# A hybrid encoder block on one core: first token tile ahead at the step into the MLP, a shared start of four up-projection blocks, and a last sum partly on TensorE

## The chip, the cores and the metric

The kernel runs as one program on one core of a Trainium2 chip. The metric is the device time of one execution in microseconds (us). TensorE is called PE in the rows below (PEld is its weight load), VectorE DVE, ScalarE ACT, GpSimd POOL, SyncE SP.

## The reference

One residual block is computed for 256 tokens of 2048 channels. It has three sub-layers, each with a norm before it (scale each token by the inverse root mean square) and a norm of its result before the residual sum: token mixers (gated DeltaNet and pooling), cross-attention into 256 memory tokens, and a gated MLP. The change touches the end of the second and the third:

```python
y = memory_cross_attention(h, m, w_xq, w_xkv, w_xo)     # last step: o @ w_xo
x = x + rms_norm(y, xa_post_norm)
h = rms_norm(x, ffn_pre_norm)
u = causal_dwconv(h @ w_up, ffn_conv_w) + ffn_conv_b    # w_up: 2048 x 11008
a, b = jnp.split(u, 2, axis=-1)
y = (jax.nn.silu(a) * b) @ w_down                       # w_down: 5504 x 2048
x = x + rms_norm(y, ffn_post_norm)
```

## The kernel before

All products take float32 data that is split into two parts of fewer bits (a high and a low one); a product is then two or three matmuls. Weights are loaded by SP in chunks of 128 x 2048 (`raw`, three buffers). ACT copies the high part of 1024 columns (`whi`, L154) and DVE subtracts it (`wlo`, L155); of each part there are three buffers, so that this runs ahead of TensorE by at most three pieces of 1024 columns. Each engine takes its instructions in one order that was fixed when the program was built. A scheduler chose that order, except for instructions that are given to `pin`, which stay in the order in which the code writes them.

`proj_tm` makes a block of 512 output channels for both tiles of 128 tokens, three matmuls of 512 columns for each 128 input channels (L195 to L197). The four output blocks of cross-attention are made by it (`xo0` to `xo3`), and after each `PostNorm.block` squares the product on ACT with a sum for each token (L276) and multiplies it by the gain on DVE (L381). After the fourth, `scales` takes the sum to the power -0.5 on POOL (L393, L395), and `piece` adds the residual in quarters of 512 channels on DVE (L400), into `py_xa`. `transpose_in` turns each quarter into channel-major form by 8 transposes on TensorE (L246, two PSUM tiles `tp_h`), and ACT and DVE read these tiles, ACT for the high and DVE for the low part (L253, L255), into `h3T`. That gives the input of the MLP's up-projection in four quarters.

`proj_cm` makes a block of 128 channels of the up-projection for all 256 tokens: 16 pairs of matmuls of 512 and 256 columns (L171, L174). `up` takes blocks in the order 0, 43, 1, 44 and so on (`ua` and `ub`), and adds, scales by the token factors `R3`, convolves, and multiplies. The token factors come from eight squares of `py_xa` (`j_h`), one power for each token tile and a matmul that spreads them over the partitions (`Rp`, then `R`). PSUM has four tiles for the products of `proj_tm` and `proj_cm` (pool `acc`) and four for all else.

The last block of the down-projection, `dn3`, has `tail=3`: over its last six rows of 128 channels the first token tile goes first, and `ff_end` for it runs under the second one's matmuls. `ff_end` for the second tile ends the program with four pieces on DVE and their stores.

Of the kernel before, what the change touches and what calls it, by code (L numbers as in the profile page):

```python
# [25 lines left out]
def kernel(  # L26
    ctx: ExitStack,
    tc: tile.TileContext,
    x: bass.AP,          # [256, 2048]
    x_cm: bass.AP,       # [2, 128, 8, 256]  x, channel-major  # L30
    mem_cm: bass.AP,     # [2, 128, 8, 256]
    w_cm: bass.AP,       # [57, 128, 2048]   (q,k,v per head; b/a; p), channel-major blocks
    w_z: bass.AP,        # [4, 128, 16, 512]
    w_ga: bass.AP,       # [4, 128, 16, 512]
    w_gb: bass.AP,       # [4, 128, 16, 512]
    w_ya: bass.AP,       # [4, 128, 16, 512]
    w_yb: bass.AP,       # [4, 128, 8, 512]
    w_mo: bass.AP,       # [4, 128, 16, 512]
    w_pool: bass.AP,     # [128, 2048]       (c | group, out block, in block, d)
    w_xq: bass.AP,       # [16, 128, 2048]  # L40
    w_xk: bass.AP,       # [16, 128, 2048]
    w_xv: bass.AP,       # [4, 128, 16, 512]
    w_xo: bass.AP,       # [4, 128, 16, 512]
    w_up: bass.AP,       # [86, 128, 2048]
    w_dn: bass.AP,       # [4, 128, 43, 512]
    conv_w: bass.AP,     # [128, 48, 4]
    ffn_w: bass.AP,      # [128, 86, 3]
    ffn_b: bass.AP,      # [128, 86]
    pregain: bass.AP,    # [128, 4, 16]      (mix, xa, mem, ffn)
    postgain: bass.AP,   # [3, 128, 2048]  # L50
    gdn_gain: bass.AP,   # [128, 1]
    pool_sc: bass.AP,    # [128, 8]
    ab: bass.AP,         # [16, 2]           (a_log, dt_bias)
    c_ident: bass.AP,    # [128, 128]
    c_le: bass.AP,       # [128, 128]        1 where partition <= column
    c_gt: bass.AP,       # [128, 128]        1 where partition > column
    c_tinit: bass.AP,    # [128, 256]
    c_invc: bass.AP,     # [128, 64]
    out: bass.AP,        # [256, 2048]
# [126 lines left out]
    def proj_tm(wsrc, X, KT, name, tail=0, mid=None):  # L186
        """out [128 tokens, 512] for both token tiles; over the last 2 * tail rows of
        128 the first token tile goes first, and mid(its product) follows it."""
        ps = [ps_acc(f"tm{t}_{name}") for t in range(NT)]

        def mm(t, k, wh, wl):
# [1007 lines left out]
```

## Time and profile before

| what | value |
|---|---|
| time, median of 3 runs | 2026.81 us (2026.27 to 2026.9) |
| span of the profiled execution, first to last instruction | 2026.0 us |
| PE busy | 2001.8 us, 99% of the span |
| DVE, ACT busy | 1386.6 us (68%), 1099.6 us (54%) |
| mean granted TensorE clock | 0.997 of full speed |
| chain that ended last, by engine | PE 95%, DVE 1% |

The span is that of the one profiled execution; what lies around it is 0.3 to 0.9 us by the three timed runs. Granted clock 1.00 is 2.4 GHz and 0.50 is 1.2 GHz. Busy times overlap, so that shares do not add up to one. A matmul's duration in a row reaches beyond the start of the next one, since matmuls are pipelined.

### The profile page before, as it was taken

What the parts mean: (1) busy time and instruction counts of PE and PEld (TensorE: products, weight loads), DVE (VectorE), ACT (ScalarE), POOL (GpSimd) and SP (SyncE); (2) the same over time, 40 slices, a digit from 0 to 9 for tenths busy, and PEclk for the clock granted to TensorE, in tenths of its full rate; (3) what the DMA queues carried; (4) which work ended last, traced back from release to release, by engine and by line L of the source; (5) the groups of instructions that cost most, each with busy time, mean ns of one, the idle gap of its engine ahead of it and who ended that gap; (6) DMA issues with size and microseconds to landing.
All of it is one profiled execution on the core that took longest, in us unless ns stands there. A gap on an engine that the chain in (4) does not pass through costs nothing.

```text
span 2026.0 us, 27927 instructions
## 1 busy us (share of the span) xinstructions
PE 2001.8 (99%) x10842; PEld 1703.1 (84%) x10842; DVE 1386.6 (68%) x2171; ACT 1099.6 (54%) x1826; POOL 108.5 (5%) x154
## 2 busy tenths in 40 slices
PE   8999999999999999999999999999999999999998
PEld 6888888888878888888888888788888888888886
DVE  7869687697756855678555554688888887854444
ACT  7657666566654544456444444565555555544443
POOL 1510200201100000001000000100000000000000
PEclk9999999999999999999999999999999999999999
DMA  6445354444444656456555455555555555565553
GB/s 242 166 167 183 132 184 147 160 173 146 166 170 153 236 193 249 173 199 228 185 190 175 159 207 190 204 209 187 190 189 192 193 193 187 187 231 200 188 196 141
DMA packets 55029, 377.87 MB, mean 187 GB/s; under 512 B 6768, under 2 KB 7536, under 8 KB 10224
## 3 DMA queue, kind: packets, MB, share of 16 engines
q1 hardware_dynamic: 52128, 359.73, 51.0%
q0 software_dynamic: 2192, 15.73, 2.0%
q8 instruction: 85, 1.39, 0.3%
q10 hardware_dynamic: 576, 0.62, 0.1%
q14 instruction: 48, 0.39, 0.1%
HBM read 369.77 MB, written 6.29 MB: 186 GB/s over the span
## 4 chain that ended last, share of the span: by engine, by line
PE 95%; DVE 1%; POOL 0%; ACT 0%; issue 0%; DVEq 0%; POOLq 0%; ACTq 0%
PE cm_ub L171 8%; PE cm_ua L171 8%; PE cm_ub L174 4%; PE cm_ua L174 4%; PE tm_dn L197 4%; PE tm_dn L196 4%; PE tm_dn L195 4%; PE cm_xk L171 3%; PE cm_xq L171 3%; PE cm_vg L171 3%; PE cm_kg L171 2%; PE cm_qg L171 2%; PE tm_gb L195 2%; PE cm_xk L174 1%; PE cm_xq L174 1%; PE tm_gb L196 1%
## 5 line engine op out<-in xcount | busy, mean ns | idle before, releaser
L171 PE MATMUL cm_ua<-h3T,whi_ua 128*128 128x512 f32 x688 | 242.0, 395 | 0.0
L171 PE MATMUL cm_ub<-h3T,whi_ub 128*128 128x512 f32 x688 | 241.0, 394 | 0.0
L174 PE MATMUL cm_ua<-h3T,wlo_ua 128*128 128x256 f32 x688 | 191.0, 278 | 0.0
L174 PE MATMUL cm_ub<-h3T,wlo_ub 128*128 128x256 f32 x688 | 190.7, 277 | 0.1
L155 DVE TENSOR_TENSOR wlo_dn<-raw_dn,whi_dn 128x1024 fp32r<-128x1024 f32 (+1 forms) x88 | 105.6, 1200 | 119.0 <-ACT whi_dn L154 118.8
L154 ACT CAST whi_dn<-raw_dn 128x1024 fp32r<-128x1024 f32 (+1 forms) x88 | 91.1, 1035 | 136.9 <-PE tm_dn L197 132.2
L171 PEld LDWEIGHTS cm_ua<-h3T,whi_ua 128*128 128x128 f32 x688 | 129.3, 188 | 29.8 <-ACT h3T L253 0.2
L171 PEld LDWEIGHTS cm_ub<-h3T,whi_ub 128*128 128x128 f32 x688 | 129.1, 188 | 29.9
L155 DVE TENSOR_TENSOR wlo_ub<-raw_ub,whi_ub 128x1024 fp32r<-128x1024 f32 x86 | 105.3, 1225 | 58.1 <-ACT whi_ub L154 58.0
L154 ACT CAST whi_ub<-raw_ub 128x1024 fp32r<-128x1024 f32 x86 | 90.4, 1051 | 100.3 <-issue 51.5
L154 ACT CAST whi_ua<-raw_ua 128x1024 fp32r<-128x1024 f32 x86 | 90.6, 1053 | 99.2 <-PE cm_ub L171 47.5
L195 PE MATMUL tm_dn<-whi_dn,gT 128*128 128x512 f32 x344 | 133.8, 389 | 0.0
L196 PE MATMUL tm_dn<-wlo_dn,gT 128*128 128x512 f32 x344 | 133.8, 389 | 0.0
L197 PE MATMUL tm_dn<-whi_dn,gT 128*128 128x512 f32 x344 | 133.8, 389 | 0.0
L174 PEld LDWEIGHTS cm_ub<-h3T,wlo_ub 128*128 128x128 f32 x688 | 129.2, 188 | 0.4 <-DVE wlo_ub L155 0.4
L174 PEld LDWEIGHTS cm_ua<-h3T,wlo_ua 128*128 128x128 f32 x688 | 129.5, 188 | 0.0
L155 DVE TENSOR_TENSOR wlo_ua<-raw_ua,whi_ua 128x1024 fp32r<-128x1024 f32 x86 | 105.3, 1225 | 26.6 <-ACT whi_ua L154 26.5
L171 PE MATMUL cm_vg<-uT,whi_vg 128*128 128x512 f32 x256 | 95.1, 409 | 0.0
L171 PE MATMUL cm_kg<-uT,whi_kg 128*128 128x512 f32 x256 | 93.7, 406 | 0.0
L171 PE MATMUL cm_xk<-meT,whi_xk 128*128 128x512 f32 x256 | 89.7, 396 | 0.0
L171 PE MATMUL cm_xq<-h2T,whi_xq 128*128 128x512 f32 x256 | 88.8, 394 | 0.0
L171 PE MATMUL cm_qg<-uT,whi_qg 128*128 128x512 f32 x240 | 86.4, 401 | 0.0
(412 smaller groups left out, 5350.2 us busy)
## 6 DMA issues: line engine op xcount, KB each, us to landing
raw_ua<-in_w_up_dram SPq DMA_DIRECT2D x43, 1024.0 KB, 4.8
raw_ub<-in_w_up_dram SPq DMA_DIRECT2D x43, 1024.0 KB, 4.8
raw_dn<-in_w_dn_dram SPq DMA_DIRECT2D x40, 1024.0 KB, 4.7
raw_zg<-in_w_z_dram SPq DMA_DIRECT2D x16, 1024.0 KB, 4.8
raw_ga<-in_w_ga_dram SPq DMA_DIRECT2D x16, 1024.0 KB, 4.8
raw_gb<-in_w_gb_dram SPq DMA_DIRECT2D x16, 1024.0 KB, 4.7
raw_ya<-in_w_ya_dram SPq DMA_DIRECT2D x16, 1024.0 KB, 4.8
raw_mo<-in_w_mo_dram SPq DMA_DIRECT2D x16, 1024.0 KB, 4.7
```

Source lines behind the costliest of these rows:

```text
L154: pin(nc.scalar.copy(hi[:, :m], raw[:, s:s + m]), keep)
L155: pin(nc.vector.tensor_tensor(out=lo[:, :m], in0=raw[:, s:s + m], in1=hi[:, :m].bitcast(F32), op=ALU.subtract), keep)
L171: nc.tensor.matmul(ps, lhsT=hi[:, j * P:(j + 1) * P], rhs=xk.rearrange("p a s -> p (a s)"), start=(kt == 0), stop=False)
L174: nc.tensor.matmul(ps[:, 0:S], lhsT=lo[:, j * P:(j + 1) * P], rhs=xk[:, 0, :], start=False, stop=(kt == 15))
L195: nc.tensor.matmul(ps[t], lhsT=xh, rhs=wh, start=(k == 0), stop=False)
L196: nc.tensor.matmul(ps[t], lhsT=xh, rhs=wl, start=False, stop=False)
L197: nc.tensor.matmul(ps[t], lhsT=xl, rhs=wh, start=False, stop=(k == KT - 1))
```

## The change

The loop over the output blocks of cross-attention ends after three. The weights of the first three shared pieces of the up-projection (`up_split`, each 512 columns of two blocks) are then loaded and split, and the fourth block `xo3` is made with `tail=3`. `first_token_tile` normalises the first token tile after its last matmul, and `late` puts its transposes ahead of the last six matmuls of the second. The up-projection's blocks 0, 43, 1 and 44 (`FIRST_UP`) are then made together, quarter by quarter of `h3T`, in four PSUM tiles `cm_up_st0` to `cm_up_st3`; in the first quarter each token tile has its own split and its own matmuls. The squares for the token factors stand after all four quarters. Nearly all of it is pinned. In `ff_end` of the second token tile, the first 512 channels are summed by two matmuls and copied by ACT; DVE keeps three pieces. `square_sum`, `block` and `piece` get an argument `keep` that pins them. Comments and docstrings are removed.

```diff
+    def proj_tm(wsrc, X, KT, name, tail=0, mid=None, late=None):
...
-        def mm(t, k, wh, wl):
+        def mm(t, k, wh, wl, keep=False):
...
-            nc.tensor.matmul(ps[t], lhsT=xh, rhs=wh, start=(k == 0), stop=False)
+            pin(nc.tensor.matmul(ps[t], lhsT=xh, rhs=wh, start=(k == 0), stop=False), keep)
...
         if tail:
             parts = list(chunks(K0, KT))
             for t in range(NT):
-                for part in parts:
-                    for args in part:
-                        mm(t, *args)
+                for i, p in enumerate(parts):
+                    for args in p:
+                        mm(t, *args, keep=True)
                     tick()
+                    if t and late and i == tail - 2:
+                        late()
                 if t == 0:
                     mid(ps[0])
         return ps
...
     pn = PostNorm(1, lambda t: x1[t * P:(t + 1) * P, :], "xa")
-    for nb in range(4):
+    for nb in range(3):
         pn.block(proj_tm(w_xo[nb], A, 16, f"xo{nb}"), nb)
...
     x2 = dram.tile([S, D], F32, name="x2")
-    pn.scales()
     ss = new_ss("h3")
-    h3T = []
-    for q in range(4):
-        ys = [pn.piece(t, q) for t in range(NT)]
-        d = xtile(f"h3T{q}")
-        transpose_in(d, lambda t: ys[t], pre_sb[:, 3, 4 * q:4 * q + 4], f"h3{q}")
-        h3T.append(d)
+    h3T = [xtile(f"h3T{q}") for q in range(4)]
+    H3 = getX(h3T)
+
...
+    FIRST_UP = (0, KFF, 1, KFF + 1)
+    up_parts = []
+
+    def up_split(half):
+        raw = wp.tile([P, 2048], F32, tag="raw", name=f"raw_up_st{half}")
+        c = half // 2
+        for b in range(2):
+            nc.sync.dma_start(raw[:, b * 512:(b + 1) * 512],
+                              w_up[FIRST_UP[2 * (half % 2) + b]][:, c * 512:(c + 1) * 512])
+        hl = b8(f"wup_st{half}", F32R)
+        hi, lo = hl[:, 0:1024], hl[:, 1024:2048]
+        pin(nc.scalar.copy(hi, raw[:, 0:1024]))
+        pin(nc.vector.tensor_tensor(out=lo, in0=raw[:, 0:1024], in1=hi.bitcast(F32),
+                                    op=ALU.subtract))
+        up_parts.append((hi, lo))
+
+    h3tp = {}
...
+    def h3_transpose(q, t):
+        for pr in range(2):
+            if (q, pr) not in h3tp:
+                h3tp[q, pr] = ps_g(f"tp_h3{q}_{pr}")
+            for kk in range(2):
+                o = kk * S + t * P
+                c = q * 512 + (2 * pr + kk) * P
+                pin(nc.tensor.transpose(h3tp[q, pr][:, o:o + P], pn.y[t][:, c:c + P], ident))
+
...
+    def h3_split(q, lo, hi):
+        for k in range(4):
+            gk = pre_sb[:, 3, 4 * q + k:4 * q + k + 1]
+            src = h3tp[q, k // 2][:, k % 2 * S + lo:k % 2 * S + hi]
+            d = h3T[q][:, k]
+            pin(nc.scalar.activation(d[:, 0, lo:hi], src, AF.Identity, scale=gk))
+            pin(nc.vector.scalar_tensor_tensor(out=d[:, 1, lo:hi], in0=src, scalar=gk,
+                                               in1=d[:, 0, lo:hi].bitcast(F32),
+                                               op0=ALU.mult, op1=ALU.subtract))
+
+    def first_token_tile(ps):
+        pn.block([ps] * 2, 3, [0], True)
+        pn.scales([0])
+        pn.piece(0, 0, True)
...
+    ps_up = []
+    def up_mm(half, toks):
+        c = half // 2
+        hi, lo = up_parts[half]
+        for b in range(2):
+            p2 = ps_up[2 * (half % 2) + b].rearrange("p (a s) -> p a s", a=2)
+            for k in range(4):
+                kt = 4 * c + k
+                xk = H3(kt)
+                w = slice(b * 512 + k * P, b * 512 + (k + 1) * P)
+                pin(nc.tensor.matmul(p2[:, :, toks], lhsT=hi[:, w], rhs=xk[:, :, toks],
+                                     start=(kt == 0 and toks.start == 0), stop=False))
+                pin(nc.tensor.matmul(p2[:, 0, toks], lhsT=lo[:, w], rhs=xk[:, 0, toks],
+                                     start=False, stop=(kt == 15)))
+            tick()
+
+    for half in range(3):
+        up_split(half)
+    ps = proj_tm(w_xo[3], A, 16, "xo3", 3, first_token_tile, lambda: h3_transpose(0, 0))
+    ps_up.extend(ps_acc(f"cm_up_st{i}") for i in range(4))
+    h3_split(0, 0, P)
+    pn.piece(0, 1, True)
+    for half in range(2):
+        up_mm(half, slice(0, P))
+    pn.block(ps, 3, [1], True)
+    pn.scales([1])
+    pn.piece(1, 0, True)
+    h3_transpose(0, 1)
+    h3_split(0, P, S)
+    for half in range(2):
+        up_mm(half, slice(P, S))
+    for q in range(1, 4):
         for t in range(NT):
-            square_sum(ys[t], ss[t][:, q:q + 1], f"h3{t}{q}")
+            if t or q > 1:
+                pn.piece(t, q, True)
+            h3_transpose(q, t)
+        h3_split(q, 0, S)
+        for half in (2 * q, 2 * q + 1):
+            if half + 1 < 8:
+                up_split(half + 1)
+            up_mm(half, slice(0, S))
     for t in range(NT):
         nc.gpsimd.dma_start(x2[t * P:(t + 1) * P, :], pn.y[t])
-    H3 = getX(h3T)
+        for q in range(4):
+            square_sum(pn.y[t][:, q * 512:(q + 1) * 512], ss[t][:, q:q + 1], f"h3{t}{q}",
+                       True)
...
     R3, _ = row_factors(ss, "h3")
...
     def up(blk, name):
-        ps = proj_cm(w_up[blk], H3, name)
+        if blk in FIRST_UP:
+            ps = ps_up[FIRST_UP.index(blk)]
+        else:
+            ps = proj_cm(w_up[blk], H3, name)
         xp = next_xp()
...
     def ff_end(t, ps):
         pn.block([ps] * 2, 3, [t])
         pn.scales([t])
+        if t:
+            po = ps_g("last")
+            nc.tensor.matmul(po, lhsT=ident, rhs=pn.x[1][:, 0:512], start=True, stop=False)
+            dr = tmp.tile([P, P], F32, tag="t", bufs=3, name="dr")
+            nc.scalar.activation(dr, ident, AF.Identity, scale=pn.r[1][:, 0:1])
+            nc.tensor.matmul(po, lhsT=dr, rhs=pn.y[1][:, 0:512], start=False, stop=True)
         for q in range(4):
-            y = pn.piece(t, q)
+            if t and q == 0:
+                y = tmp.tile([P, 512], F32, tag="j512", name="y_last")
+                nc.scalar.copy(y, po)
+            else:
+                y = pn.piece(t, q)
             eng = nc.sync if q % 2 == 0 or t == 0 else nc.scalar
             eng.dma_start(out[t * P:(t + 1) * P, q * 512:(q + 1) * 512], y)
```

The order of the built programs shows what moved. On ACT, at the step from `xo2` to `xo3`, there stood before (`whi_xo3_0_0` is the high part of the first 1024 weight columns of `xo3`, `j_xa20` and `j_xa21` are the squares of the products of `xo2` for the two token tiles):

```order
L154 CAST whi_xo2_12_1024_11343<-raw_xo2_12_11337 128x1024
L154 CAST whi_xo3_0_0_11385<-raw_xo3_0_11383 128x1024
L154 CAST whi_xo3_0_1024_11389<-raw_xo3_0_11383 128x1024
L276 ACTIVATE j_xa20_11371,pss_xa0_10926<-tm0_xo2_11233 128x512
L276 ACTIVATE j_xa21_11374,pss_xa1_10927<-tm1_xo2_11234 128x512
L154 CAST whi_xo3_4_0_11419<-raw_xo3_4_11417 128x1024
```

and now:

```order
L154 CAST whi_xo2_12_1024_11343<-raw_xo2_12_11337 128x1024
L278 ACTIVATE j_xa20_11371,pss_xa0_10926<-tm0_xo2_11233 128x512
L278 ACTIVATE j_xa21_11374,pss_xa1_10927<-tm1_xo2_11234 128x512
L1082 CAST wup_st0_11391<-raw_up_st0_11388 128x1024
L1082 CAST wup_st1_11397<-raw_up_st1_11394 128x1024
L1082 CAST wup_st2_11403<-raw_up_st2_11400 128x1024
L154 CAST whi_xo3_0_0_11410<-raw_xo3_0_11408 128x1024
L154 CAST whi_xo3_0_1024_11414<-raw_xo3_0_11408 128x1024
```

The three shared pieces stand ahead of the first piece of `xo3`, and the two squares, which need the last matmuls of `xo2`, stand ahead of these; DVE has the same order for the low parts.

On PE, in the step into the MLP, before (`tp_h31_0` is the first PSUM tile of quarter 1, `py_xa0` the first token tile, `cm_ua0` the product of block 0):

```order
L246 MATMUL tp_h31_1_11571<-ident_82,py_xa0_10922 128x128
L246 MATMUL tp_h31_1_11571<-ident_82,py_xa1_10923 128x128
L171 MATMUL cm_ua0_11666<-h3T0_11536,whi_ua0_0_11669 128x512
L174 MATMUL cm_ua0_11666<-h3T0_11536,wlo_ua0_0_11670 128x256
L171 MATMUL cm_ub0_11718<-h3T0_11536,whi_ub0_0_11721 128x512
L246 MATMUL tp_h32_0_11587<-ident_82,py_xa0_10922 128x128
L171 MATMUL cm_ua0_11666<-h3T0_11536,whi_ua0_0_11669 128x512
L174 MATMUL cm_ua0_11666<-h3T0_11536,wlo_ua0_0_11670 128x256
L246 MATMUL tp_h32_1_11596<-ident_82,py_xa0_10922 128x128
```

and now, at the step from quarter 0 to quarter 1:

```order
L1127 MATMUL cm_up_st3_11562<-h3T0_11384,wup_st1_11397 128x128
L1096 MATMUL tp_h31_0_11655<-ident_82,py_xa0_10922 128x128 x2
L1096 MATMUL tp_h31_1_11658<-ident_82,py_xa0_10922 128x128 x2
L1096 MATMUL tp_h31_0_11655<-ident_82,py_xa1_10923 128x128 x2
L1096 MATMUL tp_h31_1_11658<-ident_82,py_xa1_10923 128x128 x2
L1125 MATMUL cm_up_st0_11559<-h3T1_11385,wup_st2_11403 128x512
L1127 MATMUL cm_up_st0_11559<-h3T1_11385,wup_st2_11403 128x256
```

Before, matmuls of one quarter stood between the transposes of the next ones; now all products of a quarter stand ahead of the next quarter's transposes, and the products of that quarter directly behind them.

On DVE, at the last quarter, before (`s1_h30` sums the squares of a token tile, `dg_h30` puts its factor on a diagonal, `ua_ua0` adds up the product of block 0):

```order
L266 TENSOR_REDUCE s1_h31_11647<-nss_h31_11533 128x1
L155 TENSOR_TENSOR wlo_ub0_1024_11726<-raw_ub0_11719,whi_ub0_1024_11725 128x1024
L255 SCALAR_TENSOR_TENSOR h3T3_11611<-tp_h33_0_11612,pre_sb_80,h3T3_11611 128x256
L255 SCALAR_TENSOR_TENSOR h3T3_11611<-tp_h33_1_11621,pre_sb_80,h3T3_11611 128x256
L302 TENSOR_SCALAR dg_h30_11643<-ident_82,rstd_h30_11638 128x128
L302 TENSOR_SCALAR dg_h31_11651<-ident_82,rstd_h31_11646 128x128
L307 COPY R_h3_11636<-Rp_h3_11637 128x256
L155 TENSOR_TENSOR wlo_ua1_0_11776<-raw_ua1_11773,whi_ua1_0_11775 128x1024
L155 TENSOR_TENSOR wlo_ua1_1024_11780<-raw_ua1_11773,whi_ua1_1024_11779 128x1024
L184 TENSOR_TENSOR ua_ua0_11709<-cm_ua0_11666,t_ua0_11710 128x256
```

and now:

```order
L1105 SCALAR_TENSOR_TENSOR h3T3_11387<-tp_h33_0_11783,pre_sb_80,h3T3_11387 128x256 x2
L1105 SCALAR_TENSOR_TENSOR h3T3_11387<-tp_h33_1_11786,pre_sb_80,h3T3_11387 128x256
L155 TENSOR_TENSOR wlo_ua2_0_11932<-raw_ua2_11929,whi_ua2_0_11931 128x1024
L1105 SCALAR_TENSOR_TENSOR h3T3_11387<-tp_h33_1_11786,pre_sb_80,h3T3_11387 128x256
L1083 TENSOR_TENSOR wup_st7_11805<-raw_up_st7_11802,wup_st7_11805 128x1024
L268 TENSOR_REDUCE s1_h30_11861<-nss_h30_11382 128x1
L304 TENSOR_SCALAR dg_h30_11865<-ident_82,rstd_h30_11860 128x128
L268 TENSOR_REDUCE s1_h31_11869<-nss_h31_11383 128x1
L304 TENSOR_SCALAR dg_h31_11873<-ident_82,rstd_h31_11868 128x128
L155 TENSOR_TENSOR wlo_ua2_1024_11936<-raw_ua2_11929,whi_ua2_1024_11935 128x1024
L309 COPY R_h3_11858<-Rp_h3_11859 128x256
L184 TENSOR_TENSOR ua_ua0_11888<-cm_up_st0_11559,t_ua0_11889 128x256
```

The first weight piece of the fifth block, `wlo_ua2_0`, stands inside the last quarter's split, and its second piece ahead of `R_h3` and of the sum that frees the first of the four PSUM tiles.

## Rows read from the trace of the kernel before

**Rows 1.** The page: busy time and share of the span.

```profile
PE 2001.8 (99%) x10842; PEld 1703.1 (84%) x10842; DVE 1386.6 (68%) x2171; ACT 1099.6 (54%) x1826; POOL 108.5 (5%) x154
```

**Rows 2.** Waits of PE: line, releaser, us in total, times, longest.

```profile
PE tp_h L246 <- DVE py_xa L400: 2.7, 4, 1.3
```

**Rows 3.** Timeline of PE at the step; then L174 alone over a window.

```profile
1297.32 0.39 PE L197 MATMUL tm_xo<-whi_xo,aT 128*128 128x512 f32 x1
...
1303.02 0.78 PE L171 MATMUL cm_ua<-h3T,whi_ua 128*128 128x512 f32 x1
...
1297.55:1329.24 31.69, 17.97 (x64) 0.95 0.62 232
```

**Rows 4.** L171 in steady state: length, PE busy (count), PEclk, DMA share, GB/s.

```profile
1400.00:1500.00 100.00, 100.00 (x290) 1.00 0.55 190
```

**Rows 5.** All PE in windows around the step, columns as in rows 4.

```profile
1297.50:1301.50 4.00, 1.62 (x11) 1.00 0.79 260
1301.50:1305.00 3.50, 3.34 (x14) 0.52 0.01 5
1305.00:1310.00 5.00, 4.80 (x34) 0.99 0.29 120
```

**Rows 6.** Timeline of PE at the kernel's start.

```profile
9.63 0.58 PE L174 MATMUL cm_qg<-uT,wlo_q 128*128 128x256 f32 x1 [0.46 <-DVE wlo_q L155]
...
14.28 0.41 PE L174 MATMUL cm_qg<-uT,wlo_q 128*128 128x256 f32 x1
```

**Rows 7.** Timelines of PE, ACT, DVE and SP where xo3 follows xo2.

```profile
1275.79 0.39 PE L195 MATMUL tm_xo<-whi_xo,aT 128*128 128x512 f32 x1
...
1275.99 0.60 ACT L276 ACTIVATE j_xa<-tm_xo 128x512 f32<-128x512 f32 x1 [0.67 <-PE tm_xo L197]
...
1276.57 1.04 ACT L154 CAST whi_xo<-raw_xo 128x1024 fp32r<-128x1024 f32 x1
...
1277.64 1.22 DVE L155 TENSOR_TENSOR wlo_xo<-raw_xo,whi_xo 128x1024 fp32r<-128x1024 f32 x1
1279.80 1.22 DVE L155 TENSOR_TENSOR wlo_xo<-raw_xo,whi_xo 128x1024 fp32r<-128x1024 f32 x1 [0.93 <-ACT whi_xo L154]
...
1281.05 0.33 SPq L141 DMA_DIRECT2D raw_ua<-in_w_up_dram  x1
```

**Rows 8.** Tile raw_xo: from issue to landing of a 128 x 2048 load.

```profile
DMA to landing us min/median/max: 4.7/4.8/5.0
```

**Rows 9.** Timeline of ACT and DVE reading two transposed tiles (h2T).

```profile
946.12 0.86 ACT L253 ACTIVATE h2T<-tp_h,pre_sb 128x256 fp32r<-128x256 f32 x2 [0.95 <-DVE h2T L255]
...
945.61 0.87 DVE L255 SCALAR_TENSOR_TENSOR h2T<-tp_h,pre_sb,h2T 128x256 fp32r<-128x256 f32 x2
946.63 0.48 DVE L255 SCALAR_TENSOR_TENSOR h2T<-tp_h,pre_sb,h2T 128x256 fp32r<-128x256 f32 x1 [0.15 <-ACT h2T L253]
```

**Rows 10.** Groups of 128 x 128 on ACT and DVE: busy us, mean ns.

```profile
L625 ACT ACTIVATE Ur_g<-m_le,g_lo 128x128 fp32r<-128x128 f32 x32 | 10.7, 394 | 0.0
...
L646 DVE SCALAR_TENSOR_TENSOR UD_g<-kq_g,nbr_g,UD_g 128x128 f32<-128x128 f32 x32 | 9.7, 345 | 0.0
```

**Rows 11.** Timeline of PE: eight transposes between matmuls.

```profile
943.05 1.04 PE L246 MATMUL tp_h<-ident,py_mx 128*128 128x128 f32 x8
943.84 0.47 PE L171 MATMUL cm_xk<-meT,whi_xk 128*128 128x512 f32 x1
```

**Rows 12.** Squares of py_xa (ns min/median/max); timeline of DVE at the factors.

```profile
L276 ACT ACTIVATE j_h<-py_xa x8: 624/645/664, 1299.3 to 1310.5; 128x512 f32<-128x512 f32 x8
...
1311.51 0.15 DVE L266 TENSOR_REDUCE s_h<-nss_h 128x1 f32<-128x4 f32 x1
...
1314.98 0.42 DVE L307 COPY R_h<-Rp_h 128x256 f32<-128x256 f32 x1 [0.66 <-PE Rp_h L304]
```

**Rows 13.** Timeline of the kernel's end, ACT and DVE.

```profile
2018.19 0.60 ACT L276 ACTIVATE j_ff<-tm_dn 128x512 f32<-128x512 f32 x1 [3.39 <-PE tm_dn L197]
...
2019.91 2.74 DVE L400 SCALAR_TENSOR_TENSOR py_ff<-py_ff,prstd_ff,px_ff 128x512 f32<-128x512 f32 x4 [0.31 <-POOL prstd_ff L395]
```

More of the change, by code (lines that the diff above doesn't have):

```diff
@@ L184, in cm_sum @@
         nc.vector.tensor_tensor(out=dst, in0=ps[:, 0:S], in1=t, op=ALU.add)
-    def proj_tm(wsrc, X, KT, name, tail=0, mid=None):
+    def proj_tm(wsrc, X, KT, name, tail=0, mid=None, late=None):
         ps = [ps_acc(f"tm{t}_{name}") for t in range(NT)]
-        def mm(t, k, wh, wl):
+        def mm(t, k, wh, wl, keep=False):
             xk = X(k)
@@ L194, in mm @@
             xl = xk[:, 1, t * P:(t + 1) * P]
-            nc.tensor.matmul(ps[t], lhsT=xh, rhs=wh, start=(k == 0), stop=False)
-            nc.tensor.matmul(ps[t], lhsT=xh, rhs=wl, start=False, stop=False)
-            nc.tensor.matmul(ps[t], lhsT=xl, rhs=wh, start=False, stop=(k == KT - 1))
+            pin(nc.tensor.matmul(ps[t], lhsT=xh, rhs=wh, start=(k == 0), stop=False), keep)
+            pin(nc.tensor.matmul(ps[t], lhsT=xh, rhs=wl, start=False, stop=False), keep)
+            pin(nc.tensor.matmul(ps[t], lhsT=xl, rhs=wh, start=False, stop=(k == KT - 1)), keep)
         def chunks(k0, k1):
@@ L271, in rstd_of, with square_sum @@
         return r
-    def square_sum(src, dst, name):
+    def square_sum(src, dst, name, keep=False):
         junk = tmp.tile([P, 512], F32, tag="j512", name=f"j_{name}")
-        nc.scalar.activation(junk, src, AF.Square, accum_out=dst)
+        pin(nc.scalar.activation(junk, src, AF.Square, accum_out=dst), keep)
     def pre_norm(src, gi, name, tiles, ss):
@@ L375, in __init__, with block @@
             self.r = []
-        def block(self, ps, nb, ts=range(NT)):
+        def block(self, ps, nb, ts=range(NT), keep=False):
             sl = slice(nb * 512, (nb + 1) * 512)
             for t in ts:
-                square_sum(ps[t], self.ss[t][:, nb:nb + 1], f"{self.name}{nb}{t}")
-                nc.vector.tensor_tensor(out=self.y[t][:, sl], in0=ps[t], in1=self.g[:, sl],
-                                        op=ALU.mult)
+                square_sum(ps[t], self.ss[t][:, nb:nb + 1], f"{self.name}{nb}{t}", keep)
+                pin(nc.vector.tensor_tensor(out=self.y[t][:, sl], in0=ps[t],
+                                            in1=self.g[:, sl], op=ALU.mult), keep)
             if nb == 2:
@@ L396, in scales, with piece @@
                 self.r.append(r)
-        def piece(self, t, q):
+        def piece(self, t, q, keep=False):
             sl = slice(q * 512, (q + 1) * 512)
-            nc.vector.scalar_tensor_tensor(
+            pin(nc.vector.scalar_tensor_tensor(
                 out=self.y[t][:, sl], in0=self.y[t][:, sl], scalar=self.r[t][:, 0:1],
-                in1=self.x[t][:, sl], op0=ALU.mult, op1=ALU.add)
+                in1=self.x[t][:, sl], op0=ALU.mult, op1=ALU.add), keep)
             return self.y[t][:, sl]
```

## The prediction

> **What bounds the kernel now.** I read the page first: PE is busy for 2001.8 us of 2026.0 [rows 1], so the other engines matter only where PE waits for them. The waits of PE come next. At the place of the change there is one, 2.7 us before the transposes `tp_h` [rows 2]; the join of `xo2` and `xo3`, which the change touches too, has none. The timeline of PE tells what the step into the MLP costs in all. The last matmul of `xo3` starts at 1297.32, and PE is free some 0.23 us later, at 1297.55. By 1329.24, 31.69 us on, the 64 pairs of the first four blocks are done [rows 3]. In steady state 290 pairs take 100 us [rows 4], 0.345 each, which makes 22.1; 32 transposes at 0.1 (eight delay the next matmul by 0.79 [rows 11]) make 3.2; the factor matmuls, four such passes, 0.4. That is 25.7, so the step loses **6.0 us**. Part of it is the clock: it is granted at 0.52, its lower level of 1.2 GHz, for 3.5 us after PE had been busy for only 1.62 of 4.00 us [rows 5]. Half of 3.5, 1.7, is lost to it, the rest to waits and gaps. 6.0 us is all that the step can give back, 0.3% of the time.
>
> **The join of xo2 and xo3.** The change puts the splits of three shared pieces ahead of those of `xo3`, and they stand behind the two squares of `xo2`. The second square needs the last matmul of `xo2`; it starts at 1275.99 and the next ACT instruction at 1276.57 [rows 7]. Now the weights of `xo3` are ready by then, and PE goes on at 1275.79. In the changed order that instruction is the cast of the first shared piece, until 1277.61, and the subtraction follows on DVE, which is at its place at 1277.64 too, until 1278.86 [rows 7]. The three buffers `raw` are then all held by shared pieces, so the first load of `xo3` needs this subtraction to end. SP issues such a load 0.03 us behind its release (1279.80 and 1.22, then 1281.05 [rows 7]): 1278.9. It lands 4.8 later [rows 8], at 1283.7; the cast (1.04) takes it to 1284.75, the subtraction (1.22) to 1286.0. PE can do two matmuls with the high part before that, and goes on at 1286.05. That is 10.3 us after 1275.79, less two matmuls of 0.23: **+9.8**. Behind this wait are all matmuls of `xo3`, and nobody else has work to fill it. The range is narrow: the landing goes from 4.7 to 5.0, and I allow 1 us for the next loads in flight. Less than 8 only comes if the loads don't wait for the splits.
>
> After such a pause PE starts at the lower clock. The one stretch in rows 5 lasted 3.5 us; at the kernel's start a matmul of 256 columns still took 0.41 at 14.28, where 64 of them take 0.28 on average [rows 3], 4.65 us after 9.63 [rows 6]. Half of 3.5 to 4.65 is 1.7 to 2.3; I take **+2.1**.
>
> **The step itself.** The change is to let the first token tile's work run under the second one's matmuls. But in the new order PE does a quarter's transposes, and then the products that need their split, with nothing between. The split goes through ACT and DVE in turns: ACT starts 0.51 behind DVE's start on the same tile (945.61, 946.12), and DVE 0.51 behind ACT's (946.63) [rows 9]. In the pinned order (two channel blocks of the first PSUM tile, then two of the second) the starts from the first ACT read on are: ACT 0, DVE 0.51, ACT 1.02, DVE 1.53, DVE again 1.93 (a DVE pair takes 0.87 in rows 9, so 0.40 behind), ACT 2.44, DVE 2.95, done at 3.47. The first read starts about 0.83 behind the first transpose (six of eight fill the first tile, and the last must arrive; an estimate from 0.1 each). So the fourth pair of the first block starts at 4.3. Three pairs fit in before; 13 follow, 4.49. A quarter takes 8.79 where 6.32 (0.8 and 16 pairs) is work: 2.47 of waiting, in each of quarters 1 and 2.
>
> The first quarter goes by token tile. With 128 columns the reads take 0.39 and 0.35 [rows 10], with the 0.04 between engines of rows 9 steps of 0.43 and 0.39, and the chain 2.75 behind 0.43. Its matmuls of 256 and 128 columns take 0.12 and, by the nearest row, the transposes', 0.1; I take 0.2 for both. 2.75, 0.43 and 13 pairs of 0.2 make 5.78 for each token tile. From the first early transpose on, quarter 0 ends at 11.6, quarter 1 at 20.4, quarter 2 at 29.1.
>
> In the last quarter the weight piece `wlo_ua2_0` stands inside the split: a cast and a subtraction, of which some 1.0 us delays the last pair. So the four blocks are done at 38.9. Next late are the factors. ACT starts its last read of the split 0.83 and 2.69 after 29.14, at 32.7; it casts the last shared piece from 33.0 to 34.0, and then does eight squares of 0.645 [rows 12], to 39.1. From the sum of the squares to the copy of `R` it took 3.47 [rows 12]: 42.6. Copy and first sum on DVE, 0.42 each, free the PSUM tile that the fifth block needs: 43.5. (The squares' place costs nothing before, where they lie between reads; their cover is gone here, and PE waits 4.6 us.) 1.4 of the 43.5 are the last six matmuls of `xo3`, so the step takes 42.1 against 31.7: **+10.4**. From below, with the half pairs as cheap as whole ones (0.17) and POOL faster at the factors by 1, it is 8; from above, with every pinned wait 0.1 longer, 13.
>
> The Trainium skill, in PSUM — Partial Sum Buffer, section "PSUM bank collisions raise a hardware error", asks that two engines that use one bank be kept apart by semaphores, readers too. Rows 9 agree: the 0.95 of idle ACT time there ended with DVE. If both could read one bank together, the chain would be 2.2 in place of 3.47 and 1.7 in place of 2.75, and the sum 5.9 lower; I go by the row.
>
> The clock in the step: 4.6 us of waiting before the fifth block is more than what brought it down in rows 5, so I count one fall, **+1.7**. None would be 0; one at each quarter too, four in all, 6.8.
>
> **The end.** DVE has three pieces in place of four; four take 2.74 [rows 13], so 0.68 less. The quarter that moved goes: factor at 2019.9, a scaled identity on ACT (0.39 [rows 10]), a float32 matmul of 512 columns (no row; four times a pass of 0.1, twice, 0.8), a copy like the square of 512 columns, 0.60 [rows 13]. With handovers it ends at about 2022.0, as the third piece does. **-0.6**; if the matmul takes twice that, 0.
>
> **Sum.** 9.8 + 2.1 + 10.4 + 1.7 - 0.6 = 23.4. Against the profiled span of 2026.0 that is 2049.4; the median lies 0.8 above that span, so 2050.2. I predict **2050**.
>
> **Rivals.** *The change does what it is for.* If loads of `xo3` come early and splits keep up with PE, the step's 6.0 and the end's 0.6 come back: 2020.2. For it: the tail of `dn3` is built alike and has no PE wait. Against: both orders. It decides if PE's wait at the join is under 1 us and that in each quarter under 0.5. *Only the join waits*, and the splits hide: 9.8 + 2.1 - 6.0 - 0.6, 2032. It needs the reads of two engines to overlap nearly whole, against rows 9. *Only the step waits*, since `xo3` is loaded into buffers that I think held: 10.4 + 1.7 - 0.6, 2038. *The clock falls in every quarter*: 5.1 more, 2055, and with slower chains 2060. For it: in each quarter PE works for under half of some 4 us; against: rows 5 show a fall only after longer idleness than that. *The change does nothing that counts*, gains and waits within 4 us of each other: nothing in the rows speaks for it.
>
> **Numbers.** Forecast 56 in 100 (2044 to 2055 with its bounds), clock in every quarter 15, only the step 9, only the join 10, faster 6, no change 4. The first three make 80, from 2037 to 2060. What a measurement of this kernel can tell from no change is about 0.2%, 4 us. Faster by more: 6 in 100; within: 4; slower: 90.
>
> **What would show it.** Right: PE waits for the cast and the subtraction of `xo3` once, 9 to 10 us; each shared quarter shows PE waiting for DVE's split (L1105), 2 to 3 us; PE waits for DVE's first sum (L184) before block 2, 3 to 5 us; the granted clock is half behind the first and the last of these. Wrong: a load of `xo3` issued before the last matmul of `xo2`; quarters of 6.5 us; squares that end under the fourth block; a granted clock of 1 throughout.

## The result, and the profile after

The changed kernel takes **2059.89 us** (median of four executions, 2051.4 to 2062.88) against 2026.67 for the kernel before on the same chip: the ratio is 1.0155 [1.014, 1.0169]. It is slower, as forecast, by 33 us where 23.4 were forecast. The four times do not form one group. The profiled execution took 2051.4 (span 2049.7), 1.4 us from the forecast; the other three took 2059.5 to 2062.9. A repeat, below, gave a profile of the second kind.

The spans of the profiled executions, cut at four PE rows that each trace has (the last start of `xo2`, of `xo3`, the first of the fifth block `cm_ua` and the last of `dn3`):

| stretch | before | after | after, repeat |
|---|---|---|---|
| to the last start of `xo2` | 1275.56 | 1274.91 | 1275.92 |
| join and `xo3` | 21.76 | 34.47 | 34.90 |
| step, to the fifth block | 31.92 | 43.39 | 43.47 |
| other 82 blocks, down-projection | 688.53 | 688.68 | 697.43 |
| last matmul to the end | 8.22 | 8.25 | 8.24 |
| span | 2026.0 | 2049.7 | 2060.0 |

Busy time by engine on the page of the profiled execution, beside [rows 1]; PE was busy for 10.1 us longer with 36 matmuls more. Part of that is the lower clock, at which a matmul of 512 columns lasted 0.63 to 0.80 in place of 0.39 (rows below):

```profile
PE 2011.9 (98%) x10878; PEld 1711.2 (83%) x10878; DVE 1387.7 (68%) x2174; ACT 1101.8 (54%) x1832; POOL 106.7 (5%) x154
```

The waits of PE in it (us in total, times, longest), beside [rows 2]:

```profile
PE tm_xo L195 <- ACT whi_xo L154: 9.1, 1, 9.1
PE cm_up_st L1125 <- DVE h3T L1105: 7.7, 13, 1.4
PE last L1200 <- ACT dr L1199: 1.4, 1, 1.4
PE cm_ua L171 <- DVE ua_ua L184: 1.3, 1, 1.3
```

The join, in the timelines of PE, ACT, DVE and SP of the same execution (start, length; in brackets the idle time before and its releaser), beside [rows 7]:

```profile
1274.91 0.39 PE L197 MATMUL tm_xo<-whi_xo,aT 128*128 128x512 f32 x1
1284.38 1.22 PE L195 MATMUL tm_xo<-whi_xo,aT 128*128 128x512 f32 x2 [9.07 <-ACT whi_xo L154]
1285.63 0.79 PE L196 MATMUL tm_xo<-wlo_xo,aT 128*128 128x512 f32 x1
...
1289.21 0.63 PE L196 MATMUL tm_xo<-wlo_xo,aT 128*128 128x512 f32 x1
1289.64 0.47 PE L197 MATMUL tm_xo<-whi_xo,aT 128*128 128x512 f32 x1
...
1275.93 2.93 ACT L1082 CAST wup_st<-raw_up_st 128x1024 fp32r<-128x1024 f32 x3
1283.28 1.99 ACT L154 CAST whi_xo<-raw_xo 128x1024 fp32r<-128x1024 f32 x2 [4.43 <-DMA raw_xo<-in_w_xo_dram]
...
1276.99 3.50 DVE L1083 TENSOR_TENSOR wup_st<-raw_up_st,wup_st 128x1024 fp32r<-128x1024 f32 x3
...
1278.25 8.82 SPq L141 DMA_DIRECT2D raw_xo<-in_w_xo_dram  x4
```

ACT and DVE go to the shared pieces behind the squares of `xo2`; the first subtraction ends at about 1278.2, and SP issues the first load of `xo3` at 1278.25. It lands 5.0 later, and PE has stood for 9.07 us. Then a matmul of 512 columns takes 0.63, until 1289.64 with 0.47: PE works at the lower clock for 5.3 us.

A shared quarter, in the timelines of PE, ACT and DVE:

```profile
1321.61 1.05 PE L1096 MATMUL tp_h<-ident,py_xa 128*128 128x128 f32 x8
1323.52 0.50 PE L1125 MATMUL cm_up_st<-h3T,wup_st 128*128 128x512 f32 x1 [0.87 <-DVE h3T L1105]
...
1324.55 0.50 PE L1125 MATMUL cm_up_st<-h3T,wup_st 128*128 128x512 f32 x1 [0.41 <-DVE h3T L1105]
...
1325.96 0.50 PE L1125 MATMUL cm_up_st<-h3T,wup_st 128*128 128x512 f32 x1 [0.40 <-DVE h3T L1105]
...
1330.58 1.04 PE L1096 MATMUL tp_h<-ident,py_xa 128*128 128x128 f32 x8
...
1322.47 0.47 ACT L1104 ACTIVATE h3T<-tp_h,pre_sb 128x256 fp32r<-128x256 f32 x1 [5.93 <-PE tp_h L1096]
1323.50 0.84 ACT L1104 ACTIVATE h3T<-tp_h,pre_sb 128x256 fp32r<-128x256 f32 x2 [0.55 <-DVE h3T L1105]
1324.92 0.47 ACT L1104 ACTIVATE h3T<-tp_h,pre_sb 128x256 fp32r<-128x256 f32 x1 [0.58 <-DVE h3T L1105]
...
1325.42 0.48 DVE L1105 SCALAR_TENSOR_TENSOR h3T<-tp_h,pre_sb,h3T 128x256 fp32r<-128x256 f32 x1 [0.54 <-ACT h3T L1104]
```

The quarter takes 8.97 us (1321.61 to 1330.58; 8.79 was forecast). ACT stands for DVE's read twice, half a microsecond each, and PE waits three times for the split, 1.7 us in all. The end of the step, and where the clock fell within it (PE's timeline, the long matmuls are those at half speed, and a row of DVE):

```profile
1307.76 0.63 PE L1096 MATMUL tp_h<-ident,py_xa 128*128 128x128 f32 x4
...
1309.38 0.40 PE L197 MATMUL tm_xo<-whi_xo,aT 128*128 128x512 f32 x1
...
1316.98 0.50 PE L1125 MATMUL cm_up_st<-h3T,wup_st 128*128 128x256 f32 x1 [0.34 <-DVE h3T L1105]
...
1320.37 0.41 PE L1125 MATMUL cm_up_st<-h3T,wup_st 128*128 128x256 f32 x1
...
1344.99 0.80 PE L1125 MATMUL cm_up_st<-h3T,wup_st 128*128 128x512 f32 x1 [1.43 <-DVE h3T L1105]
...
1347.72 0.44 PE L1125 MATMUL cm_up_st<-h3T,wup_st 128*128 128x512 f32 x1
...
1350.89 0.61 PE L306 MATMUL Rp_h<-dg_h,ones 128*128 128x128 f32 x4
1352.77 0.50 PE L171 MATMUL cm_ua<-h3T,whi_ua 128*128 128x512 f32 x1 [1.27 <-DVE ua_ua L184]
...
1352.30 0.41 DVE L184 TENSOR_TENSOR ua_ua<-cm_up_st,t_ua 128x256 f32<-128x256 f32 x1
```

### The profile page after: what moved, and what is told of

The parts are those of the page before. It is cut to its first block, busy times and chain, and to the rows that moved or that the text cites. A ratio compares the mean times of both kernels' runs of the same rounds, so it can differ in the third digit from the quotient of the medians.

```text
span 2049.7 us, 28023 instructions
## 1 busy us (share of the span) xinstructions
PE 2011.9 (98%) x10878; PEld 1711.2 (83%) x10878; DVE 1387.7 (68%) x2174; ACT 1101.8 (54%) x1832; POOL 106.7 (5%) x154
## 4 chain that ended last, share of the span: by engine, by line
PE 95%; DVE 2%; ACT 1%; DMA 1%; issue 0%; POOL 0%; SPq 0%; POOLq 0%; ACTq 0%; DVEq 0%
PE cm_ua L171 7%; PE cm_ub L171 7%; PE tm_dn L196 4%; PE cm_ub L174 4%; PE cm_ua L174 4%; PE tm_dn L195 4%; PE tm_dn L197 4%; PE cm_xk L171 3%; PE cm_xq L171 3%; PE cm_vg L171 3%; PE cm_kg L171 3%; PE cm_qg L171 3%; PE tm_gb L195 1%; PE tm_xo L196 1%; PE tm_xo L195 1%; PE cm_xk L174 1%
## 5 line engine op out<-in xcount | busy, mean ns | idle before, releaser
L171 PE MATMUL cm_ua<-h3T,whi_ua 128*128 128x512 f32 x656 | 229.3, 391 | 1.3 <-DVE ua_ua L184 1.3
L171 PE MATMUL cm_ub<-h3T,whi_ub 128*128 128x512 f32 x656 | 229.2, 391 | 0.0
L174 PE MATMUL cm_ub<-h3T,wlo_ub 128*128 128x256 f32 x656 | 183.7, 280 | 0.0
L174 PE MATMUL cm_ua<-h3T,wlo_ua 128*128 128x256 f32 x656 | 183.7, 280 | 0.0
L171 PEld LDWEIGHTS cm_ua<-h3T,whi_ua 128*128 128x128 f32 x656 | 122.7, 187 | 28.3 <-DVE ua_ua L184 1.5
L171 PEld LDWEIGHTS cm_ub<-h3T,whi_ub 128*128 128x128 f32 x656 | 122.7, 187 | 26.9
L155 DVE TENSOR_TENSOR wlo_ub<-raw_ub,whi_ub 128x1024 fp32r<-128x1024 f32 x82 | 100.4, 1225 | 54.2 <-ACT whi_ub L154 54.0
L174 PEld LDWEIGHTS cm_ub<-h3T,wlo_ub 128*128 128x128 f32 x656 | 124.0, 189 | 0.0
L174 PEld LDWEIGHTS cm_ua<-h3T,wlo_ua 128*128 128x128 f32 x656 | 124.0, 189 | 0.0
L155 DVE TENSOR_TENSOR wlo_ua<-raw_ua,whi_ua 128x1024 fp32r<-128x1024 f32 x82 | 100.5, 1225 | 23.4 <-ACT whi_ua L154 23.4
L171 PE MATMUL cm_vg<-uT,whi_vg 128*128 128x512 f32 x256 | 94.3, 407 | 0.0
L171 PE MATMUL cm_kg<-uT,whi_kg 128*128 128x512 f32 x256 | 93.6, 405 | 0.6 <-ACT whi_kg L154 0.6
L171 PE MATMUL cm_xk<-meT,whi_xk 128*128 128x512 f32 x256 | 89.8, 396 | 0.0
L171 PE MATMUL cm_xq<-h2T,whi_xq 128*128 128x512 f32 x256 | 88.8, 394 | 0.0
L171 PE MATMUL cm_qg<-uT,whi_qg 128*128 128x512 f32 x240 | 86.6, 402 | 0.0
```

The costliest lines, as they stand in the source:

```text
L155: pin(nc.vector.tensor_tensor(out=lo[:, :m], in0=raw[:, s:s + m], in1=hi[:, :m].bitcast(F32), op=ALU.subtract), keep)
L171: nc.tensor.matmul(ps, lhsT=hi[:, j * P:(j + 1) * P], rhs=xk.rearrange("p a s -> p (a s)"), start=(kt == 0), stop=False)
L174: nc.tensor.matmul(ps[:, 0:S], lhsT=lo[:, j * P:(j + 1) * P], rhs=xk[:, 0, :], start=False, stop=(kt == 15))
```

## Experiments

**The same kernel again.** No edit, five rounds.

> The changed kernel once more, unchanged, to see which of its four times (2051.4 in the execution with the profile, 2059.5 to 2062.9 in the others) is the usual one, and what fills the difference. Theory: the same waits stand in each execution (9.1 us at the join, 12.0 in the step), and what varies is the granted clock behind them, since each of the four pauses leaves it near its fall; then the times spread over 2050 to 2063, and a slower execution shows longer stretches at 0.5 between 1310 and 1360 and nothing else. Rival: the extra 8 to 11 us lie in the products behind the step (the up-projection or the last product), where nothing of the order is changed; then the stretch from the fifth block to the last matmul is longer than 688.7 us.

2049.84, 2052.43, 2061.18, 2061.66 and 2064.48; ratio 1.0147 [1.0121, 1.0172]. Six of nine executions in all lie in the upper group. The profiled one has a span of 2060.0, and the rival holds: its step is as long as the first's, its blocks behind it are 8.75 us longer (the table). PE waits for nothing in them. A pair is one matmul of 512 columns (L171) and one of 256 (L174). First and last pair of the stretch in the repeat:

```profile
1354.29 0.50 PE L171 MATMUL cm_ua<-h3T,whi_ua 128*128 128x512 f32 x1 [1.05 <-DVE ua_ua L184]
...
1817.61 0.40 PE L171 MATMUL cm_ub<-h3T,whi_ub 128*128 128x512 f32 x1
```

and the last one in the first profile (its first is the 1352.77 above):

```profile
1807.37 0.39 PE L171 MATMUL cm_ub<-h3T,whi_ub 128*128 128x512 f32 x1
```

Both stretches hold 1312 pairs (82 blocks of 16), 1311 steps: 463.32 us make **353.4 ns** a pair, 454.60 make **346.8**. The difference, 8.7 us, is most of the 10.3 between the two spans; 1.0 lies ahead of the last start of `xo2`, 0.4 in the join and 0.1 in the step. L171 takes 398 ns (median) in place of 391; the granted clock is 1.00 in both. The other seven executions have no profile: that the five others of the upper group have the slower pace is concluded from their times.

**The join undone.** The first two shared pieces behind the splits of `xo3`, the third behind the first quarter's split.

```diff
             parts = list(chunks(K0, KT))
+            if pre:
+                pre()
...
-    for half in range(3):
-        up_split(half)
-    ps = proj_tm(w_xo[3], A, 16, "xo3", 3, first_token_tile, lambda: h3_transpose(0, 0))
+    ps = proj_tm(w_xo[3], A, 16, "xo3", 3, first_token_tile, lambda: h3_transpose(0, 0),
+                 lambda: [up_split(half) for half in range(2)])
...
     h3_split(0, P, S)
+    up_split(2)
```

> The changed kernel with the loads and splits of the first two shared pieces behind those of xo3 and the third behind the first quarter's split; everything else as in the change. Theory (the pieces ahead of xo3 cost a wait of 9.1 us and 3.1 us of low clock and waiting behind it): the wait of PE for whi_xo is gone, the time falls by 12, to 2038 to 2048, and the step stays at 43 us from the last matmul of xo3 to the fifth block. Rival (the load of xo3 is late for another reason, the queue for example): the wait stays above 5 us and the time within 4 us of the changed kernel's. Second rival: the shared pieces now come late in their turn, and PE waits for wup_st instead, 3 us or more.

2038.19, 2038.24, 2047.21, 2049.06; ratio 1.0078 [1.0057, 1.01]. The wait is gone, and the clock does not fall there; the profiled execution, at 346.7, has a span of 2036.4, 13.3 under 2049.7. The join and `xo3` take 23.44 in place of 34.47, 11.0 less; a new wait has come to stand in them, that of the early transposes for the first token tile:

```profile
PE tp_h L1098 <- DVE py_xa L404: 1.0, 1, 1.0
```

The step keeps its waits for the split (7.7 in 13) and takes 41.74, with one fall of the clock in place of two. The times still lie in two groups, some 9 us apart, so the join is not what makes them.

**Alternating tiles.** `for k in range(4)` in `h3_split` becomes `for k in (0, 2, 1, 3)`.

> The changed kernel with one line changed: the four channel blocks of a quarter are split in the order 0, 2, 1, 3, so that ACT and DVE are at different PSUM tiles at a time. Theory (the alternation of two engines on one tile makes the chain 3.42 us long): the chain from ACT's first read to DVE's last write falls to 2.4 in each of quarters 1 to 3 and by about 0.8 in each half of quarter 0, PE's wait for the split (7.7 us in all) to 3 to 4.5, and the time by 3 to 5 us, more by 1 to 3 if a fall of the clock goes with it. Rival (each read waits for the other engine's hand-over, not for its tile): the chain stays at 3.4 and the time within 1 us as far as the spread lets that be seen.

2046.7, 2047.61, 2055.15, 2056.02; ratio 1.0119 [1.0101, 1.0137]. One quarter in the timelines of ACT and DVE:

```profile
1319.29 0.84 ACT L1104 ACTIVATE h3T<-tp_h,pre_sb 128x256 fp32r<-128x256 f32 x2 [4.58 <-PE tp_h L1096]
1320.31 0.86 ACT L1104 ACTIVATE h3T<-tp_h,pre_sb 128x256 fp32r<-128x256 f32 x2 [0.19 <-DVE h3T L1105]
...
1320.82 0.88 DVE L1105 SCALAR_TENSOR_TENSOR h3T<-tp_h,pre_sb,h3T 128x256 fp32r<-128x256 f32 x2 [0.15 <-ACT h3T L1104]
```

From ACT's first read to DVE's end are 2.41 us (1319.29 to 1321.70) in place of 3.43 (1322.47 to 1325.90, DVE's last subtraction). The step takes 38.87 in place of 43.47 in the repeat. By my estimate 1.7 of that, half of 3.4 us at the lower clock, is a fall of the clock that is not there, and the other 2.9 come with the shorter chains. PE's waits for the split are longer, though fewer: 6.4 us in 8, not the 3 to 4.5 that I expected, because the second block of a quarter now comes third. The Trainium skill, in PSUM — Partial Sum Buffer, section "PSUM bank collisions raise a hardware error", wants engines on one bank held apart and lets them work on two at once; the trace agrees: an idle ACT of 0.55 on the same tile, 0.19 on alternate ones.

**The end alone**, in the kernel before.

> The kernel before with the last edit of the change alone: the first quarter of the second token tile is summed by TensorE and copied out by ACT. Predicted: 0.6 us less. By the changed kernel's profile: the last store is issued 4.7 us behind the last product in place of 5.3, but the span's end lies 8.25 behind it in place of 8.23, so 0. Theory now: within 0.3 us of the kernel before, because the landing of the last store, not its issue, ends the span. Rival: 0.5 to 0.8 us less, the profile of the changed kernel having had a slow last store by chance.

2027.37 against 2027.37; ratio 1.0001 [0.9992, 1.0009]. A total cannot show 0.6 us at that width; the trace can say where it goes. Issues in this kernel (KB each, median us to landing):

```profile
out_dram<-py_ff SPq DMA_DIRECT2D x5, 256.0 KB, 2.2
out_dram<-y_last SPq DMA_DIRECT2D x1, 256.0 KB, 2.7
```

Counted from the last product's start, the last store is issued 0.55 us sooner than before and takes 2.67 to land where it took 2.27, so it lands only 0.15 sooner. That is no chance: in every profile with this edit, the changed kernel's included, the last store takes 2.6 to 3.3. That the stores, now closer together, delay each other is a guess.

**Four passes between pairs.** Two float32 matmuls, result unused, behind `ub4`, whose own matmuls are pinned with them.

```diff
+        if i == 4:
+            junk = ps_g("reset")
+            for t in range(NT):
+                pin(nc.tensor.matmul(junk[:, t * P:(t + 1) * P], lhsT=ones, rhs=ident,
+                                     start=True, stop=True))
```

> The changed kernel with two float32 matmuls of 128 columns (four passes, 0.4 us, their result unused) between the blocks ub4 and ua5. The repeat showed that the pairs behind the step take 346.7 ns in some executions and 353.3 in others, from the first pair after the last wait of PE to the last pair, 1311 pairs, 8.7 us. Theory A: the moment at which PE starts again after a wait for another engine chooses the pace, and pairs without a wait keep it; in the kernel before, the four passes of the factors lie between pairs with no wait, and behind them the pace is always 346.7. Then the passes put in here set it to 346.7 behind ub4, and all executions lie within 2 us of each other, at 2050 to 2053. Rival B: the pace of an execution is fixed by something else (addresses, the state of the chip), or the passes don't touch it: two groups again, near 2051 and 2060. Rival C: such passes choose anew, but freely: two groups.

2050.08, 2052.29, 2052.36, 2052.51; ratio 1.0119 [1.0104, 1.0135]: one group. In this profile the pace changes at the passes. PE's timeline:

```profile
1356.29 0.40 PE L171 MATMUL cm_ua<-h3T,whi_ua 128*128 128x512 f32 x1
...
1369.01 0.40 PE L171 MATMUL cm_ua<-h3T,whi_ua 128*128 128x512 f32 x1
...
1386.68 0.60 PE L1191 MATMUL reset<-ident,ones 128*128 128x128 f32 x4
...
1390.24 0.40 PE L171 MATMUL cm_ua<-h3T,whi_ua 128*128 128x512 f32 x1
...
1402.72 0.40 PE L171 MATMUL cm_ua<-h3T,whi_ua 128*128 128x512 f32 x1
```

36 pairs lie between the first two rows and between the last two: 353.3 ns each ahead of the passes, 346.7 behind.

**The squares early.** Two or four of them at the end of each quarter's loop, not all eight behind it.

> The changed kernel with the eight squares of the step moved ahead: those of quarters 0 to 2 behind the weight casts of quarters 1 and 2, two behind the last. Theory (they stand before the factors and the sums that free the fifth block's PSUM tile): PE's wait of 1.0 to 1.3 us for the first sum (ua_ua) goes, the step is 1.2 to 1.6 us shorter at the same pace, executions near 2050 or near 2059. Rival: the wait stays, because the sums themselves (a copy on ACT, 0.37, and an addition, 0.42, behind the last pair) set it, or the squares delay the weight casts and PE waits for wup_st instead.

2047.1, 2047.8, 2051.26, 2052.63; ratio 1.011 [1.0096, 1.0124]. The wait before the fifth block is gone and the step takes 42.03, 1.4 less. Here too the pairs behind the step run at 346.7 and no execution is near 2059, which I had not expected: now nothing waits between the factors' four passes and the pairs. PE's timeline:

```profile
1353.66 0.60 PE L306 MATMUL Rp_h<-dg_h,ones 128*128 128x128 f32 x4
1354.02 0.47 PE L171 MATMUL cm_ua<-h3T,whi_ua 128*128 128x512 f32 x1
```

**All of it reordered.** Join undone, alternating tiles, early squares, and each quarter's transposes and split ahead of the products of the quarter before.

```diff
     for q in range(1, 4):
+        if q < 3:
+            for t in range(NT):
+                h3_transpose(q + 1, t)
+            h3_split(q + 1, 0, S)
...
         for half in (2 * q, 2 * q + 1):
+            if half + 2 < 8:
+                up_split(half + 2)
             up_mm(half, slice(0, S))
```

> The change in the order that it would need: the shared pieces split behind xo3's, the transposes and the split of each quarter ahead of the products of the quarter before it, the channel blocks in the order 0, 2, 1, 3, the squares early. Theory (the waits at the join and for the split, the factors' wait and the falls of the clock behind them are the whole loss): PE waits for the split under 2 us in all in place of 7.7, no fall of the clock in the step; from the version with the join undone (2036.4 span at the fast pace) 7.7, 1.2, 1.0 and 1.7 come off and up to 2 stay: 2025 to 2029 at 346.7 ns a pair, 2034 to 2038 at 353.3. Rival (the forecast's rival, the change does what it is for): 2020 to 2022 at the fast pace. Rival: DVE, with the split, two pieces and two weight subtractions for each quarter (6 us where PE's work is 6.3), becomes the bound, and over 4 us of waiting stay.

2030.23, 2039.43, 2041.03, 2041.05; ratio 1.0052 [1.0031, 1.0072]. No wait for the split is left; but 1.7 for weight pieces, 1.6 for transposes, 1.1 for the first sum and one fall of the clock are. The step takes 34.21. I had expected 2025 to 2029 at the faster pace and no fall of the clock. With the four passes added:

> The version before this one with the four passes between ub4 and ua5 as well. Theory A of the pace: all executions at 2025 to 2029, which is the kernel before or 1 us around it. Rivals B and C: two groups, 8 to 9 us apart.

2030.91 to 2033.89 in five executions and 2039.71 in a sixth; ratio 1.003 [1.0018, 1.0043]. I had expected 2025 to 2029 for all. The sixth has no profile; why it is longer stays open. The profiled one runs at 346.7 ahead of the passes too, so this version does not show them change the pace.

**Its last waits taken away.** The shared pieces of a quarter come in one buffer (`up_load`, four loads of 512 columns), and the sums of the first two blocks stand behind their last products.

```diff
+            if half == 6:
+                for n in range(2):
+                    first_sum(n)
```

> The reordered version (e_pipe) with its last waits taken away: the shared pieces of a quarter are loaded together into one buffer, so that the last piece no longer lands 4 us late, and the sums of the first two blocks stand ahead of the fifth block's weight splits. Theory: the waits for wup_st (0.9 and 0.8) and for the first sum (1.1) go, and the fall of the clock behind them (1.7), so 2028.5 less 4.4 is a span of 2024.1, 2025.8 us, 1 to 2 us under the kernel before; and since no wait is left between the four passes of the factors and the pairs behind them, the pairs run at 346.7 ns in every execution. Rival: two groups 8 to 9 us apart again, so a wait of PE is still there or the passes are not what sets the pace. Rival: the quarters' splits now collide with the fifth block's, PE waits 3 us or more, and the time is 2029 or more.

2026.27 to 2027.68 in eleven executions, one group; ratio **0.9996 [0.9987, 1.0005]**. Waits of PE in the step:

```profile
PE tp_h L1102 <- DVE py_xa L404: 0.7, 1, 0.7
...
PE cm_up_st L1133 <- DVE wup_st L1090: 0.5, 1, 0.5
```

The granted clock stays at 1.00 through the step, which takes 30.05, 1.9 less than before. Two other stretches take most of that back: the join and `xo3` are 0.6 longer than before, and the end is 0.66 longer, where the last store takes 3.3 us to land.

**Waits put back.** Into that version, ahead of `ua10`, `ua20`, `ua30` and `ua40`. DVE multiplies a column of the block before by 0, and ACT adds that to one column of the next block's weights, so that PE stands until both are done.

```diff
+                nc.vector.tensor_scalar(out=z, in0=last_ps[0][:, 0:1], scalar1=0.0,
+                                        scalar2=None, op0=ALU.mult)
+                nc.scalar.activation(hi[:, 0:1], hi[:, 0:1].bitcast(F32), AF.Identity,
+                                     bias=z[:, 0:1])
```

> The version without waits (e_best, 2024.5 span, all eleven executions within 1.4 us) with four waits put back into the up-projection, ahead of ua10, ua20, ua30 and ua40: one column of the block's high weights is written once more, with a bias that DVE makes from the block before (times 0), so PE stands for some 1.5 us at each, too short for the clock to fall. Theory A: each of the four starts chooses the pace of the 20 blocks behind it (96 pairs behind the last); the profile shows windows of 346.7 and perhaps of 353.3 ns a pair, each change at one of the four places and nowhere else; executions cost 6 us for the waits and 0 to 7 for the pace, in steps of about 2.1, so they spread over several us. Rival: the pace stays at 346.7 throughout, executions within 1.5 us of each other; then a wait alone does not change the pace.

2045.42, 2049.57, 2049.62, 2050.91. L177 in equal windows between the waits (length, PE busy and count, PEld, PEclk, DMA share, GB/s):

```profile
1330.00:1410.00 80.00, 80.00 (x232) 43.30 (x231) 1.00 0.56 193
1440.00:1520.00 80.00, 80.00 (x227) 42.56 (x227) 1.00 0.55 189
1560.00:1640.00 80.00, 80.00 (x232) 43.31 (x231) 1.00 0.54 185
1670.00:1750.00 80.00, 80.00 (x227) 42.51 (x227) 1.00 0.54 185
```

232 pairs, 227, 232, 227: by the starts of the matmuls 346.7 and 353.3 ns in turn, and each change lies at a wait. The waits were 3.1 us each, not 1.5, and the clock fell behind three of them. At the third it stayed at 1.00, and the pace changed all the same, so the fall is not what changes it.

## Why the prediction was right in its cause, and what its size missed

**The join: right.** 9.8 and 2.1 of clock were forecast, 11.9; the stretch grew by 12.71, of which 0.5 are the early transposes: 12.2. The load's issue follows the first shared subtraction as worked out. Undoing the join alone took 13.3 off the span: 11.0 in this stretch, 1.65 in the step, with one fall of the clock less, and 0.6 ahead of it, where nothing was changed.

**The step: the sum right by luck, since two terms were off in opposite directions.** 10.4 and 1.7 were forecast, 12.1; measured 11.47 and the 0.5 of transposes, 12.0. Quarters 1 and 2 took 8.97 and 9.05 (8.79). The half pairs cost 0.23, not the 0.2 that I took from the nearest row. The clock fell twice, not once, for 3.4 and 2.7 us of PE's work, so some 3.0 us are lost in place of 1.7 (an estimate, half of each). It fell in the first and the last quarter, not behind the wait before the fifth block, where I had put the one fall. That wait, for the factors, was 1.3 where 4.6 was forecast: counted from the first early transpose the four blocks were done at 43.1 in place of 38.9, PE having been held up by the falls and the longer quarters, and the sum that frees the PSUM tile at 45.0 in place of 43.5. That the squares stood in the way is shown by moving them: 1.4 us.

**The end: wrong.** -0.6 was forecast, by the issue of the last store; the stretch was 0.03 longer in the changed kernel and 0.15 shorter in the end alone, since the last landing became 0.4 longer.

**What the sum left out.** Its last step was the fifth block; behind it I took "in steady state 290 pairs take 100 us" as given. That is the step that failed. In the profiled execution of the upper group the pairs behind the step ran at 353.4 ns, which adds 8.7 us; six executions of nine lie in that group. These 8.7 us are most of the 9.7 between 2050.2 and the median, which lies outside 2044 to 2055, the forecast's own bounds. The profiled execution at the other pace came to 2051.4 for 2050.2 (its span to 2049.7 for 2049.4), and so near a hit owes something to the luck of the step.

**The rivals.** "The clock falls in every quarter" gave 2055 to 2060, near the median, and is wrong as a cause: in the step it fell in two places. "The change does what it is for", 2020.2, did not come even in the version with all but 1.2 us of the step's waits taken away and no fall of the clock, which is worth 0.9996. My 2020 counted 6.0 us given back and forgot a price that stands in my own step: 32 half pairs of 0.23 are 7.4 us where 16 whole ones of 0.347 are 5.6, so 1.8 of the 6.0; the 0.6 of the end did not come either. "Only the step waits" gave 2038, and that kernel, made by undoing the join, took 2038.2 at the faster pace.

## What to carry to other kernels

Work that is put ahead of a busy engine's loads takes its buffers and its place in ACT's and DVE's order: look at what the next load waits for before moving it. Two engines that read one PSUM tile in turn make a chain that PE must not stand behind; alternate the tiles, and have a stage's reads done under the products of the stage before. An overlap that halves matmuls pays for it: reckon that before its gain.

## What the runs showed of the hardware

The same pairs of matmuls of 512 and 256 columns, at a granted clock of 1.00 and with no wait, run at either of two paces, 346.7 or 353.3 ns a pair, and keep the one that they start with: over 1311 pairs that is 8.7 us. A start after a wait for another engine may bring either, in one program (the waits put back) and from one execution to the next (the repeat). Four float32 passes of 128 columns with pairs behind them and no wait between were followed by 346.7 in each profile that has them so (seven kernels, the one before included, whose factors lie between pairs). Only one of these profiles shows 353.3 ahead of the passes, and one execution without a profile, of 2039.71, is unexplained, so that the passes set the pace is likely and not shown beyond that. What in PE makes the two paces, and why such passes choose, these runs do not show.
